# Low parts of later weights made during the feed-forwards and loaded through GpSimd's queue

## The chip, the cores and the metric

One core of one Trainium2 chip runs the kernel. Its engines work side by side, each through a queue of its own in order: TensorE (PE: matmuls; PEld is its loading of the stationary operand), VectorE (DVE), ScalarE (ACT), GpSimd (POOL) and SyncE (SP), whose queue holds nothing but DMA issues. Sixteen DMA engines move the data. The metric is the device time of one execution in microseconds (us), the median over runs.

## The reference, cut to what matters

A network of four layers over 512 tokens of width 1024, all in float32. Two layers of a first block, each with four mixers and a gated feed-forward of width 2816:

```python
for l in range(2):
    h = rms_norm(x, pre_mix_g[l]);  z = h @ w_in[l]      # z is split into 18 column groups
    o_a, o_b = hgrn2(...), gla(...)                       # chunked recurrences
    o_c, o_d = mla_attention(...), gated_delta(...)
    x = x + rms_norm(concat(o_a, o_b, o_c, o_d) @ w_out[l], post_mix_g[l])
    h = rms_norm(x, pre_ffn_g[l])
    gate = causal_dwconv(h @ ffn_w_gate[l], ffn_conv_w[l])
    x = x + rms_norm((gelu(gate) * (h @ ffn_w_up[l])) @ ffn_w_down[l], post_ffn_g[l])
```

Then a second block: layer A (differential attention, with `a_w_in`) and layer B (stick-breaking attention, with `b_w_in` and the shared `w_kv_shared`), both with a small attention to a memory. The first block's output is the second's input.

## The kernel before

Every large product is made of float32 operands that are split into a high part (rounded to the matmul's fp32r format) and a low part (what is left), and takes three matmuls, high by high, high by low and low by high (`mm3`, L817). A weight comes in **views** of 128 partitions x 1024 values (512 KB). `wload` (L799) makes one ready: SP loads the raw view into a `wr` buffer (there are two), ScalarE casts it to the high part `wh` (four buffers), and VectorE subtracts, `wl = wr - wh` (four buffers). Both the cast and the subtraction read `wr`, so the next load into that buffer waits for both. TensorE spends 24 matmuls on a view of a projection.

`layer1(l)` is a layer of the first block: norm, the projections with the mixers (GDN, HGRN, GLA, MLA) between them, the output product, then `ffn`. `ffn(l, ...)` loops over 22 column blocks f of the feed-forward: two views each (gate and up), convolution and gelu on ScalarE and VectorE, and the product with `ffn_w_down` at the end. The stages of the profile below follow this: layer 0's mixers 30 to 385 us, its feed-forward loop 385 to 604 and down product 604 to 706, layer 1's mixers 726 to 1022, its feed-forward 1072 to 1422, layer A 1440 to 1706, layer B from 1731 on.

The order of the work is not the order of the code. Every operation is recorded (`Engine`; all carry the line of its call, L328), and a planner (`Plan.simulate`) walks through them with a cost for each, and lets every engine take the ready operation that comes first in the program. The operations are then emitted in the order of their planned starts. The planner has DMAs on an engine of their own; in the emitted program a DMA stands in the queue of the engine that issues it. A load that depends on nothing can be planned far ahead if a buffer of its pool is free. The pool `p2` (128x512, ten buffers, printed as `p` or `p2`) serves the mixers and the feed-forward for temporaries. The rstd of a norm is made on GpSimd: a `TENSOR_SCALAR` and a `TENSOR_TENSOR` (a power) on `st` tiles of a few values per partition.

Of the kernel before, what the change touches and what calls it, by code (L numbers as in the profile page):

```python
# [10 lines left out]
F32 = mybir.dt.float32  # L11
F32R = mybir.dt.float32r
# [12 lines left out]
NF = DFF // 128  # L25
# [122 lines left out]
def run(gen):  # L148
    for _ in gen:
        pass  # L150
# [14 lines left out]
class Clocks:  # L165
# [4 lines left out]
    def __init__(self):  # L170
        self.T = {e: 0.0 for e in ("PE", "ACT", "DVE", "POOL", "DMA")}
        self.wrote, self.read, self.slots = {}, {}, {}
# [441 lines left out]
class Net:  # L614
    def __init__(self, ctx, tc, I, out, dbg=None, upto=None):
        self.tc, self.nc, self.I, self.out, self.dbg = tc, tc.nc, I, out, dbg
        self.upto = upto
        nc = tc.nc
        self.clk = Clocks()
        self.plan = Plan(nc)  # L620
        self.plan.skip = {a.tensor.name for a in I.values()} | {out.tensor.name}
        eng = lambda name, e: Engine(self.clk, self.plan, name, e)
        self.V, self.A, self.G = eng("DVE", nc.vector), eng("ACT", nc.scalar), eng("POOL", nc.gpsimd)
        self.PE, self.SP = eng("PE", nc.tensor), eng("DMA", nc.sync)
        self.n = 0
        pool = lambda name, bufs, **k: ctx.enter_context(tc.tile_pool(name=name, bufs=bufs, **k))
        self.pc = pool("pc", 1)
        self.bufs = {"h": 8, "p": 8, "w": 16}
        self.pools = {k: pool("p4" + k, n) for k, n in self.bufs.items()}
        self.p2_ = pool("p2", 10)  # L630
        self.pst = pool("pst", 31)
        self.pst4 = pool("pst4", 10)
        self.pwr = pool("pwr", 2)
        self.pwh = pool("pwh", 4)
        self.pwl = pool("pwl", 4)
        self.pps = {"A": pool("psA", 3, space=PSUM), "S": pool("psS", 3, space=PSUM), "D": pool("psD", 2, space=PSUM)}
        self.pdr = pool("pdr", 2, space=bass.MemoryType.DRAM)
        self.turn = 0
        self.ready_w, self.mem_kv, self.mem_hT = {}, {}, {}
        self.ahead = lambda: None  # L640

    def nm(self, s):
# [156 lines left out]
    def wload(self, view, tag=None):  # L799

        if self.wkey(view) in self.ready_w:
            return self.ready_w.pop(self.wkey(view))
        sh = list(view.shape)
        raw = self.new(self.pwr, 2, sh, F32, "wr", "wr")
        for k in range(sh[1] if len(sh) == 4 else 1):
            part = (slice(None), k) if len(sh) == 4 else slice(None)
            self.SP.dma_start(out=raw[part], in_=view[part])
        if tag:
            hi, lo = (self.p4(sh, F32R, tag) for _ in range(2))
        else:  # L810
            hi = self.new(self.pwh, 4, sh, F32R, "wh", "wh")
            lo = self.new(self.pwl, 4, sh, F32R, "wl", "wl")
        self.A.copy(hi, raw)
        self.sub(lo, raw, hi.bitcast(F32))
        return hi, lo

    def mm3(self, out, a, b, start, stop):  # L817

        self.mm(out, a[0], b[0], start, False)
        self.mm(out, a[0], b[1], False, False)  # L820
        self.mm(out, a[1], b[0], False, stop)
# [1052 lines left out]
    def ffn_views(self, l):  # L1874
        I = self.I
        return [self.cols(I[k][l], f * 128, 128) for f in range(NF) for k in ("ffn_w_gate", "ffn_w_up")]

    def ffn(self, l, h, rest, then):

        I = self.I  # L1880
        Wd = I["ffn_w_down"][l]
        views = self.ffn_views(l) + [self.out_rows(Wd, 0, 0)]
        acts = []
        first = self.fm_first(h, [self.wload(v) for v in views[:3]], rest)
        self.preload(views[3])

        def proj(i):
            if i < 3:
                return first[i]
            w = self.wload(views[i])  # L1890
            self.preload(views[i + 1])
            return self.fm(h, w)

        for f in range(NF):
            if l == 0 and f == 2:
                run(self.mem_prep(1))
            psg, psu = proj(2 * f), proj(2 * f + 1)
            c = self.p2()
            self.act(c, psg, AF.Copy, scale=self.fcols[l](f, 2))
            for j in (1, 0):  # L1900
                s = 2 - j
                self.stt(c[:, s:], psg[:, :S - s], self.fcols[l](f, j), c[:, s:], ALU.mult, ALU.add)
            self.act(c, c, AF.Gelu_apprx_tanh)
            self.mul(c, psu, c)
            a = self.p4([128, 2, S], F32R, "w" if f < 16 else "p")
            self.split(a[:, 0, :], a[:, 1, :], c)
            acts.append(a)
        gb = self.bcast_row(I["post_ffn_g"][l], D)
        self.xt = self.load_x(acts[NF - 1][:, 0, :].bitcast(F32), "w")
        return self.out_proj(Wd, lambda k, t: (acts[k][:, 0, t * 128:(t + 1) * 128], acts[k][:, 1, t * 128:(t + 1) * 128]),  # L1910
                             list(range(0, NF, 2)), lambda t, ps: self.residual_norm(t, ps, gb, "w"),
                             "SSSD", "AAAD", then, "pw")
# [636 lines left out]
```

## Time and profile before

| | |
|---|---|
| median of 3 runs (lowest, highest) | 2016.34 us (2011.52, 2017.5) |
| the profiled execution | 2016.91 us, its span 2014.8 us |
| busy share of the span | PE 97%, PEld 82%, DVE 62%, ACT 47%, POOL 13% |
| the chain that ended last | PE 84%, DVE 7%, issue 3%, POOL 2%, ACT 2%, DMA 1% |
| `DVE wl` subtractions | 296, 338.5 us in all |
| DMA traffic | 195.81 MB, 97 GB/s over the span |

The profile comes from one execution. "Busy" of an engine is the sum of its instructions' times. The chain is followed back from the last instruction, at each step to what released it; a piece of it is time that the program could not do without as it stands. "Windows" give busy times of each engine in a stretch of the span. In the names, `out<-in`, numbers of buffers are left out.

### The profile page before, as it was taken

The page shows a single profiled execution, that of the slowest core. Times are in us where ns is not written, and L with a number is a line of the kernel's source. Part 1 is how long each engine was busy: PE and PEld are TensorE (multiplying, and loading weights), DVE is VectorE, ACT ScalarE, POOL GpSimd, SP SyncE. Part 2 cuts the span into 40 slices and gives each one's busy share as a digit, 9 for nine tenths or more (in the row PEclk, how much of TensorE's full clock was granted, in tenths as well). Part 3 has the DMA queues.
Part 4 walks back from the last instruction along what each step waited for, and adds up shares of the span by engine and source line. Part 5 has one row for each costly group of instructions (what it writes and reads, how often), then busy time and mean ns, then how long its engine had stood idle before and what let it go on. Part 6 is the DMA issues. An engine that isn't in the chain of part 4 may idle for free.

```text
span 2014.8 us, 33230 instructions
## 1 busy us (share of the span) xinstructions
PE 1954.8 (97%) x13254; PEld 1660.5 (82%) x13254; DVE 1250.2 (62%) x2333; ACT 948.5 (47%) x1723; POOL 260.6 (13%) x374
## 2 busy tenths in 40 slices
PE   7999999999999999998999999999999999999999
PEld 6888777888888878886887888888899988888777
DVE  8688884544442266878745444422648886558796
ACT  6654464433331246633644333322446764457782
POOL 2201211000000021011111000000323310005141
PEclk9999999999999999998999999999999999999999
DMA  7321136333332433302253333325421213322121
GB/s 222 95 64 36 62 105 200 108 100 96 95 94 94 157 110 95 77 25 64 64 189 102 97 94 95 94 94 178 136 64 54 76 62 130 121 84 63 53 74 63
DMA packets 232457, 195.81 MB, mean 97 GB/s; under 512 B 22480, under 2 KB 201328, under 8 KB 232304
## 3 DMA queue, kind: packets, MB, share of 16 engines
q1 hardware_dynamic: 232304, 193.71, 31.1%
q8 instruction: 104, 1.70, 0.4%
q14 instruction: 49, 0.40, 0.1%
HBM read 176.37 MB, written 17.30 MB: 96 GB/s over the span
## 4 chain that ended last, share of the span: by engine, by line
PE 84%; DVE 7%; issue 3%; POOL 2%; ACT 2%; DMA 1%; SPq 0%; DVEq 0%; POOLq 0%; ACTq 0%
PE psA L328 63%; PE psS L328 13%; PE psD L328 8%; DVE p4w L328 4%; POOL st L328 2%; ACT p4w L328 1%; DVE p4p L328 1%; DVE p L328 1%; DMA wr<-in_w_in_dram 1%; DVE wl L328 0%; DVE st L328 0%; DVE p4h L328 0%; DMA p4p<-in_x_dram 0%; ACT wh L328 0%; ACT p4p L328 0%
## 5 line engine op out<-in xcount | busy, mean ns | idle before, releaser
L328 DVE TENSOR_TENSOR wl<-wr,wh 128x1024 fp32r<-128x1024 f32 (+4 forms) x296 | 338.5, 1150 | 413.1 <-ACT wh L328 408.3
L328 PE MATMUL psA<-p4h,wh 128*128 128x512 f32 (+1 forms) x1952 | 585.7, 382 | 0.2 <-ACT p4h L328 0.2
L328 ACT CAST wh<-wr 128x1024 fp32r<-128x1024 f32 (+4 forms) x296 | 290.2, 989 | 486.6 <-PE psA L328 287.7
L328 PEld LDWEIGHTS psA<-p4h,wh 128*128 128x128 f32 x1952 | 359.8, 189 | 76.1 <-issue 2.5
L328 PE MATMUL psA<-p4h,wl 128*128 128x512 f32 (+1 forms) x976 | 374.7, 384 | 0.6 <-DVE wl L328 0.6
L328 PE MATMUL psA<-wh,p4h 128*128 128x256 f32 (+1 forms) x1728 | 347.0, 292 | 0.0
L328 PEld LDWEIGHTS psA<-wh,p4h 128*128 128x128 f32 x1728 | 276.3, 190 | 5.6 <-issue 2.3
L328 PE MATMUL psA<-wl,p4h 128*128 128x256 f32 (+1 forms) x864 | 249.3, 289 | 0.0
L328 PEld LDWEIGHTS psA<-p4h,wl 128*128 128x128 f32 x976 | 184.2, 189 | 34.0 <-DVE wl L328 0.8
L328 POOL TENSOR_SCALAR st<-st 128x1 f32<-128x1 f32 (+4 forms) x114 | 37.5, 329 | 1260.9 <-ACT p4w L328 841.4
L328 PEld LDWEIGHTS psA<-wl,p4h 128*128 128x128 f32 x864 | 164.5, 190 | 1.6 <-issue 0.8
L328 PE MATMUL psA<-wh,p4w 128*128 128x512 f32 (+1 forms) x540 | 162.3, 371 | 2.4 <-DVE p4w L328 1.9
L328 ACT ACTIVATE p<-p 128x512 f32<-128x512 f32 (+2 forms) x174 | 87.2, 526 | 106.9 <-DVE p L328 105.5
L328 POOL TENSOR_TENSOR st<-st,c 128x1 f32<-128x1 f32 (+4 forms) x112 | 118.9, 1063 | 8.4
L328 ACT ACTIVATE p4w<-psA 128x256 f32<-128x256 f32 (+5 forms) x138 | 61.9, 452 | 117.3 <-PE psA L328 112.8
L328 PEld LDWEIGHTS psA<-wh,p4w 128*128 128x128 f32 x540 | 97.7, 190 | 21.2 <-DVE p4w L328 2.3
L328 PE MATMUL psA<-wl,p4w 128*128 128x512 f32 (+1 forms) x270 | 99.0, 368 | 0.0
L328 DVE TENSOR_TENSOR p<-psA,p 128x512 f32<-128x512 f32 x54 | 37.3, 691 | 98.4 <-PE psA L328 93.0
L328 PE MATMUL psS<-p4w,p4w 128*64 128x64 f32 (+9 forms) x800 | 96.3, 279 | 2.0 <-DVE p4w L328 1.8
L328 PE MATMUL psS<-wh,p4w 128*128 128x512 f32 x300 | 97.4, 395 | 0.0
L328 PE MATMUL psS<-consts,p4w 128*128 128x128 f32 (+1 forms) x448 | 68.4, 285 | 26.2 <-DVE p4w L328 17.3
L328 PEld LDWEIGHTS psS<-consts,p4w 128*128 128x128 f32 x448 | 53.3, 150 | 36.4 <-DVE p4w L328 14.9
(237 smaller groups left out, 3239.1 us busy)
## 6 DMA issues: line engine op xcount, KB each, us to landing
wr<-in_w_in_dram SPq DMA_DIRECT2D x44, 512.0 KB, 3.8
wr<-in_ffn_w_gate_dram SPq DMA_DIRECT2D x44, 512.0 KB, 3.8
wr<-in_ffn_w_up_dram SPq DMA_DIRECT2D x44, 512.0 KB, 3.8
wr<-in_ffn_w_down_dram SPq DMA_DIRECT2D x44, 512.0 KB, 3.5
wr<-in_w_out_dram SPq DMA_DIRECT2D x16, 512.0 KB, 3.9
wr<-in_a_w_in_dram SPq DMA_DIRECT2D x16, 512.0 KB, 3.8
wr<-in_b_w_in_dram SPq DMA_DIRECT2D x16, 512.0 KB, 3.9
p4w<-xd SPq DMA_DIRECT2D x12, 512.0 KB, 4.6
```

The costliest lines, as they stand in the source:

```text
L328: op.fn(*op.args, **op.kw)
```

## The change

While the feed-forward of layer l runs, a new function `low_part` makes the low parts of weights that are needed after it, and stores them in DRAM; `later(l)` lists these views: all 28 of layer 1's mixers for l = 0, and 38 of A's and B's for l = 1. Each view goes in two halves of 128x512: SP loads the raw half into a `p2` buffer, ScalarE casts it into a second, VectorE subtracts into a third, and SP stores that to the DRAM tile `lw`. `wload` of such a view later still loads the raw view and casts it on ScalarE, but the low part comes from `lw` by a DMA that is issued on GpSimd (`self.G.dma_start`) straight into `wl`, in place of VectorE's subtraction. The raw buffer then has one reader, not two. The products are the same. The counts of operations change so: `wl` subtractions from 296 to 232, 132 more subtractions and casts of half views, 132 more raw loads and 132 stores on SP, 64 loads on GpSimd (two of the views stored, both of A, are not loaded again).

```diff
--- before.py
+++ after.py
@@ -636,7 +636,7 @@
         self.pps = {"A": pool("psA", 3, space=PSUM), "S": pool("psS", 3, space=PSUM), "D": pool("psD", 2, space=PSUM)}
         self.pdr = pool("pdr", 2, space=bass.MemoryType.DRAM)
         self.turn = 0
-        self.ready_w, self.mem_kv, self.mem_hT = {}, {}, {}
+        self.ready_w, self.mem_kv, self.mem_hT, self.low = {}, {}, {}, {}
         self.ahead = lambda: None
 
     def nm(self, s):
@@ -811,8 +811,25 @@
             hi = self.new(self.pwh, 4, sh, F32R, "wh", "wh")
             lo = self.new(self.pwl, 4, sh, F32R, "wl", "wl")
         self.A.copy(hi, raw)
-        self.sub(lo, raw, hi.bitcast(F32))
+        if self.wkey(view) in self.low:
+            self.G.dma_start(out=lo, in_=self.low[self.wkey(view)])
+        else:
+            self.sub(lo, raw, hi.bitcast(F32))
         return hi, lo
+
+    def low_part(self, view):
+
+        sh = list(view.shape)
+        d = self.pdr.tile(sh, F32, tag=self.nm("lw"), name=self.nm("lw"))
+        h = sh[1] // 2
+        for j in range(2):
+            a = (slice(None), slice(j * h, j * h + h))
+            raw, hi, lo = (self.new(self.p2_, 10, [128, h] + sh[2:], dt, "p2", "p2_") for dt in (F32, F32R, F32R))
+            self.SP.dma_start(out=raw, in_=view[a])
+            self.A.copy(hi, raw)
+            self.sub(lo, raw, hi.bitcast(F32))
+            self.SP.dma_start(out=d[a], in_=lo.bitcast(F32))
+        self.low[self.wkey(view)] = d
 
     def mm3(self, out, a, b, start, stop):
 
@@ -1875,6 +1892,27 @@
         I = self.I
         return [self.cols(I[k][l], f * 128, 128) for f in range(NF) for k in ("ffn_w_gate", "ffn_w_up")]
 
+    def later(self, l):
+
+        I = self.I
+        if l == 0:
+            W = I["w_in"][1]
+            gdn, gate_d = self.gdn_items(1, W, None, None, {})
+            items = gdn + gate_d + self.hgrn_items(1, W, None, {})[0] + self.gla_items(1, W, None, {})[0] + \
+                self.mla_items(1, W, None, {}) + self.hgrn_items(1, W, None, {})[1] + self.gla_items(1, W, None, {})[1] + \
+                self.mem_items(1)
+            return [v for vs, _ in items for v in vs]
+        A, K, B = I["a_w_in_2"][0], I["w_kv_shared_2"], I["b_w_in_2"][0]
+        halves = lambda W, c: [self.cols(W, c, 256)[:, k:k + 4] for k in (0, 4)]
+        out = []
+        for g in range(1, 8):
+            out += halves(A, 1536 + g * 256)
+        for g in range(3):
+            out += halves(K, 768 + g * 256)
+        for n in range(6):
+            out += [self.cols(W, c + n * 128, 128) for W, c in ((K, 0), (B, 0), (B, 1024))]
+        return out
+
     def ffn(self, l, h, rest, then):
 
         I = self.I
@@ -1891,7 +1929,10 @@
             self.preload(views[i + 1])
             return self.fm(h, w)
 
+        todo = self.later(l)
         for f in range(NF):
+            for v in todo[f * len(todo) // NF:(f + 1) * len(todo) // NF]:
+                self.low_part(v)
             if l == 0 and f == 2:
                 run(self.mem_prep(1))
             psg, psu = proj(2 * f), proj(2 * f + 1)
```

Since the planner orders all operations anew, their places in the queues change too. First SP's queue at the start of the program. The names are tiles (`p4w`: inputs of the memory's norm, `p_945` and `st`: parameters of the second block, `wr`: raw weights) with numbers of the program's own, and `in_...` the kernel's inputs. Before:

```order
L328 DMA p4w_172<-in_mem_norm_dram 128x1024
L328 DMA p4w_176<-in_mem_dram 128x1024
L328 DMA p4w_183<-in_mem_dram 128x1024
L328 DMA p_945_1040<-in_plam_dram 128x256
L328 DMA st_1044<-in_positions_dram 128x4x1
L328 DMA wr_154<-in_wsm_dram 128x8x56
L328 DMA wr_168<-in_w_in_dram 128x8x128
L328 DMA wr_191<-in_w_in_dram 128x8x128
```

And SP's queue at the same place in the changed kernel:

```order
L328 DMA p4w_172<-in_mem_norm_dram 128x1024
L328 DMA p4w_176<-in_mem_dram 128x1024
L328 DMA p4w_183<-in_mem_dram 128x1024
L328 DMA p_715_809<-in_w_in_dram 128x4x128
L328 DMA p_718_812<-in_w_in_dram 128x4x128
L328 DMA p_725_818<-in_w_in_dram 128x4x128
L328 DMA p_728_821<-in_w_in_dram 128x4x128
L328 DMA p_739_831<-in_w_in_dram 128x4x128
L328 DMA st_1240<-in_positions_dram 128x4x1
L328 DMA wr_154<-in_wsm_dram 128x8x56
L328 DMA wr_168<-in_w_in_dram 128x8x128
```

Five raw half views for layer 1, whose casts come in layer 0's feed-forward, now stand ahead of `wsm` and of the weight `wr_168` of layer 0; the 128 KB of `plam` moved to a later place. At the end of layer 0's feed-forward five half views of `a_w_in` stand in the same way, and lie in `p2` until layer 1's feed-forward.

Second GpSimd's queue where layer 0's feed-forward ends and layer 1 begins. The `st` operations are the rstds of the two norms there for the last blocks of rows; a `TENSOR_TENSOR` makes what the `TENSOR_SCALAR` of the same chain began. Before:

```order
L328 MEMSET p4w_1333 128x1024
L328 TENSOR_SCALAR st_1179<-st_1178 128x1
L328 MEMSET p4w_1334 128x1024
L328 TENSOR_TENSOR st_1180<-st_1179,c_108 128x1
L328 TENSOR_SCALAR st_1189<-st_1188 128x1
L328 TENSOR_SCALAR st_1196<-st_1193,st_1195 128x1
L328 TENSOR_TENSOR st_1190<-st_1189,c_108 128x1
L328 TENSOR_TENSOR st_1197<-st_1196,c_108 128x1
```

GpSimd's queue at the same place in the changed kernel:

```order
L328 MEMSET p4w_1529 128x1024
L328 DMA wl_1417<-lw_808 128x1024
L328 TENSOR_SCALAR st_1375<-st_1374 128x1
L328 MEMSET p4w_1530 128x1024
L328 DMA wl_1421<-lw_817 128x1024
L328 DMA wl_1426<-lw_830 128x1024
L328 TENSOR_TENSOR st_1376<-st_1375,c_108 128x1
L328 TENSOR_SCALAR st_1385<-st_1384 128x1
L328 TENSOR_SCALAR st_1392<-st_1389,st_1391 128x1
L328 TENSOR_TENSOR st_1386<-st_1385,c_108 128x1
L328 TENSOR_TENSOR st_1393<-st_1392,c_108 128x1
```

Three loads of low parts now stand among these rstds. Each has to wait until TensorE has done with the old part in its `wl` buffer, and what stands behind it on GpSimd waits with it. At the way into A two such loads stand among the rstds, and at the way into B two ahead of one rstd and two ahead of the next.

Third GpSimd's queue at the way into B in the changed kernel, where the `st` operations are again rstds of the last blocks of rows; before, they stood one behind the other.

```order
L328 DMA wl_3423<-lw_2202 128x1024
L328 DMA wl_3426<-lw_2219 128x1024
L328 TENSOR_SCALAR st_3404<-st_3403 128x1
L328 TENSOR_TENSOR st_3405<-st_3404,c_108 128x1
L328 TENSOR_SCALAR st_3410<-st_3409 128x1
L328 TENSOR_TENSOR st_3411<-st_3410,c_108 128x1
L328 DMA wl_3456<-lw_2226 128x1024
L328 DMA wl_3459<-lw_2243 128x1024
L328 TENSOR_SCALAR st_3416<-st_3415 128x1
L328 TENSOR_TENSOR st_3417<-st_3416,c_108 128x1
```

Two rstds now stand behind two loads each. TensorE's matmuls are the same ones as before; in layer 1's mixers their order changes in many places, elsewhere hardly.

## Rows read from the trace of the kernel before

**Rows 1.** The page: busy time and share; the chain that ended last, by engine

```profile
PE 1954.8 (97%) x13254; PEld 1660.5 (82%) x13254; DVE 1250.2 (62%) x2333; ACT 948.5 (47%) x1723; POOL 260.6 (13%) x374
...
PE 84%; DVE 7%; issue 3%; POOL 2%; ACT 2%; DMA 1%; SPq 0%; DVEq 0%; POOLq 0%; ACTq 0%
```

**Rows 2.** Windows by stage: length; PE, PEld, DVE, ACT, POOL busy (count); clock; DMA share; GB/s

```profile
385.00:604.00 219.00, 219.00 (x959) 179.65 (x958) 102.11 (x119) 78.58 (x100) 0.00 (x0) 1.00 0.34 101
...
726.00:1022.00 296.00, 279.93 (x2888) 241.44 (x2887) 224.96 (x444) 151.06 (x276) 40.29 (x50) 0.95 0.26 75
...
1072.00:1318.00 246.00, 245.63 (x1140) 204.66 (x1141) 116.72 (x142) 88.99 (x118) 0.74 (x2) 0.99 0.32 97
...
1440.00:1706.00 266.00, 260.71 (x1960) 242.62 (x1959) 198.35 (x486) 155.89 (x333) 67.52 (x102) 1.00 0.27 81
...
1731.00:2005.00 274.00, 272.97 (x1558) 226.76 (x1557) 196.96 (x407) 173.84 (x357) 62.87 (x64) 1.00 0.21 66
```

**Rows 3.** The chain by line, in 726 to 1022 us, then in 1440 to 1706

```profile
by line: PE psA L328 53.6%; DVE p4w L328 14.0%; PE psS L328 10.4%; PE psD L328 8.8%; issue 2.7%; POOL st L328 2.0%; ACT p4w L328 1.6%; DVE p L328 1.3%; DMA wr<-in_w_in_dram 1.3%; DVE wl L328 1.1%; ACT wh L328 0.7%; DVE st L328 0.6%; DVE p4p
...
by line: PE psA L328 65.8%; PE psS L328 12.2%; POOL st L328 4.8%; PE psD L328 4.8%; ACT p4w L328 2.5%; issue 2.4%; DVE st L328 2.3%; POOL p4w L328 1.3%; ACT p4p L328 0.9%; DVE p4w L328 0.8%; DVE p L328 0.8%; ACT wh L328 0.7%; ACT p L328 0.5
```

**Rows 4.** Groups of the page: out<-in, form, count | busy us, mean ns | idle before

```profile
L328 DVE TENSOR_TENSOR wl<-wr,wh 128x1024 fp32r<-128x1024 f32 (+4 forms) x296 | 338.5, 1150 | 413.1 <-ACT wh L328 408.3
...
L328 ACT CAST wh<-wr 128x1024 fp32r<-128x1024 f32 (+4 forms) x296 | 290.2, 989 | 486.6 <-PE psA L328 287.7
```

**Rows 5.** The chain in order of time, 722 to 734 us: start, length, what

```profile
725.21 1.01 DVE wl L328 x4
...
726.64 3.95 DMA wr<-in_w_in_dram
...
730.61 1.04 ACT wh L328
```

**Rows 6.** The chain in layer 1's mixers, and one piece of B

```profile
841.95 5.51 PE psA L328 x24
...
910.41 0.47 DVE wl L328
...
912.65 0.60 DVE wl L328
...
1001.54 0.60 DVE wl L328
...
1849.88 1.23 DVE wl L328
```

**Rows 7.** Windows at the start, columns as in the stages

```profile
15.00:20.00 5.00, 3.84 (x18) 3.58 (x18) 3.80 (x16) 4.61 (x11) 3.99 (x5) 1.00 1.05 396
20.00:25.00 5.00, 4.99 (x41) 4.75 (x39) 4.83 (x17) 4.23 (x12) 4.67 (x6) 1.00 0.69 152
```

**Rows 8.** Waits, 1072 to 1318 us: who for whom, us in total, times, longest

```profile
ACT wh L328 <- PE psA L328: 98.3, 42, 3.8
```

**Rows 9.** The chain at the start

```profile
17.25 6.64 DMA wr<-in_w_in_dram
```

**Rows 10.** SP's queue at the start: start, length of the issue, what

```profile
15.79 0.33 SPq L328 DMA_DIRECT2D p<-in_plam_dram  x1
...
16.71 0.43 SPq L328 DMA_DIRECT2D wr<-in_wsm_dram  x1
```

**Rows 11.** GpSimd in order of time, 717 to 735 us

```profile
722.55 0.19 POOL L328 TENSOR_SCALAR st<-st 128x1 f32<-128x1 f32 x1
724.27 0.96 POOL L328 MEMSET p4w<- 128x1024 f32 x1 [1.52 <-DVE p4w L328]
...
727.14 1.86 POOL L328 TENSOR_SCALAR st<-st,st 128x1 f32<-128x1 f32 x1 [0.68 <-ACT p4w L328]
728.96 1.06 POOL L328 TENSOR_TENSOR st<-st,c 128x1 f32<-128x1 f32 x2
```

**Rows 12.** SP's queue: what it waited for, us in total, times, longest

```profile
SPq L328 <- DVE p L328: 29.8, 8, 10.9
```

## The prediction

> **What bounds the kernel now.** I read the page first, for who is busy and what the chain that ended last is made of: TensorE is busy 97% of the span and holds 84% of the chain, VectorE 7%, GpSimd 2%, transfers 1% [rows 1]. So nearly all the time is matmul time, and a change that leaves the matmuls alone can win only what TensorE does not do. Then I cut the span into its stages [rows 2]. The feed-forward loops (385 to 604 and 1072 to 1318 us) have TensorE busy to the last microsecond; VectorE is at 102.11 of 219 and 116.72 of 246 us there, the DMA engines at a third. The mixers of layer 1 (726 to 1022) are different: TensorE leaves 16.1 us of 296, and VectorE, at 224.96, is busy 76%. Layer A (1440 to 1706) leaves 5.3 us, B (1731 to 2005) 1.0. Last I read the chain inside the two stages where something is left [rows 3]: in layer 1's mixers VectorE's `p4w` (the recurrences) has 14.0%, 41 us, and `DVE wl`, the instructions that the change takes out, 1.1%, 3.3 us. In A `DVE wl` is not even in the list's head, while `POOL st`, the rstds of the norms, has 4.8%, 12.8 us. The reader is to see two sizes: 64 subtractions of some 1.2 us each are 79 us of VectorE, but of these only about 5 us stand on the chain.
>
> **The change part by part.** The sum is made against the profiled execution, 2016.91 us, which lies 0.6 us above the median of the three runs, 2016.34.
>
> *Removed: 64 subtractions* (28 in layer 1's mixers, 12 in A or kept for it, 24 in B). The group's mean is 1150 ns over all forms [rows 4]; the large form takes 1.21 to 1.23 us. On the chain they stand from 725.21 on, until at 726.64 a weight load goes out that waits for the raw buffer which they free (1.43 us) [rows 5], from 910.41 to 912.65 in three pieces (1.81 us with the middle one of 0.74), at 1001.54 (0.60), and once in B (1.23) [rows 6]. That is -5.1 us at first order. Behind it lies what other VectorE instructions gain because fewer stand ahead of them: no row prices that. Its bounds are nothing and all of TensorE's idle time of layer 1's mixers and A, 16.1 + 5.3 = 21.4 us [rows 2]. I take -3, near the lower end, because the chain puts most of those stages on TensorE itself (psA 53.6% and 65.8%) [rows 3] and the chain's VectorE part is one recurrence after the other, which wait for TensorE and not for a free VectorE.
>
> *Moved: TensorE's order in layer 1's mixers.* The matmuls are the same, their order there is planned anew. I cost it at nothing, with the same bounds as above.
>
> *Added in the feed-forwards: 132 raw loads of at most 256 KB, as many casts, subtractions and stores.* A cast or subtraction of 128x512 is half of one of 128x1024, 0.50 and 0.58 us by the means [rows 4]. For 28 views in the first loop VectorE gets 56 x 0.58 = 32 us and goes to 134 of 219; for 38 in the second 76 x 0.58 = 44, to 160 of 246. ScalarE, from 78.58 and 88.99, goes to 106 and 127. A view moves 1.05 MB (in and out): 29 MB over 219 us are 134 GB/s on top of 101, 40 MB over 246 us 162 on top of 97. The start of the kernel moves 396 [rows 7]. What hides all this is that the weights run ahead: casts of the second loop wait 98.3 us, in 42 waits, for TensorE to give buffers back [rows 8]. I take 0. If the cover went, because a queue stands still longer than three views take (24 matmuls of a view are 5.51 us [rows 6], so 16.5 us), TensorE would wait for the rest.
>
> *Added at the program's start: five raw loads of 256 KB in SP's queue, ahead of `wsm` and a first-layer weight,* where 128 KB stood. The queue is full there: 15 to 20 us runs at 396 GB/s with the DMA engines wholly busy [rows 7], and the chain goes through the weight load that is issued at 17.25 and takes 6.64 us [rows 9]. 5 x 0.262 - 0.131 = 1.18 MB at 0.396 MB/us are 3.0 us; the issues alone, four more of 0.33 to 0.43 us [rows 10], are 1.5. Bounds 0 (the later load is faster by what it no longer meets) and 3.0; I take 3.0, since the DMA engines are at work without a gap until the load lands (20 to 25: share 0.69).
>
> *Added to GpSimd: 64 DMA issues.* No row has a DMA issued there. From below: SP's issues, 0.33 to 0.43 us [rows 10]. From above: GpSimd's own slowest instruction of that neighbourhood, a 128x1 `st` of 1.86 us, where the same operation takes 0.19 when nothing disturbs it [rows 11]. I take 1.0, nearest to the `MEMSET` of 128x1024 there, 0.96 us: the work is over a tile of the same shape. What is queued behind an issue are rstds, and for them wait the norms, then the transposes, then TensorE. At the way into layer 1, three issues stand between the rstds of the last two row blocks: 3.0 us, less 1.6 us that GpSimd has in hand (it ends at 730.02, the weight's cast, which the chain takes, at 731.65) [rows 5, 11], +1.4. Into A two: 2.0, less the same slack, +0.4. Into B two and two: I count half of the four, +2.0. Inside A two pairs near the head norms, whose rstds are chain there (12.8 us), half counted: +2.0. Sum +5.8; from below 0 (0.4 an issue disappears in the slack), from above 13 issues (the nine at the three entries, the four in A) of 1.86, 24 us.
>
> *Loads in place of subtractions.* A 128x1024 part must land before its matmuls, where a 512 KB load took 3.8 us (median) and its issue waits until TensorE has left the old part in one of four buffers: 16.5 us of other views lie between, so I take 0; above, see the third rival.
>
> Sum: -5.1 - 3 + 0 + 3.0 + 5.8 = +0.7, so 2017.6 us; rounded **2018**, no change that can be told: 0.3% (6 us) is about what a measurement of this kernel can tell from no change.
>
> **The rivals.**
>
> *VectorE's relief is worth more (faster).* With 64 of 296 weight subtractions gone from stages in which VectorE is 72 to 76% busy, the recurrences come sooner, and the new order of TensorE fills what is left. For it speaks that layer 1 alone loses some 33 us of VectorE work and has 16.1 us of idle TensorE; against it that `DVE wl` is 1.1% of its chain. All 21.4 us back, less 3.0 at the start and 3.0 of GpSimd: 2016.9 - 15.4 = 2001.5 us.
>
> *GpSimd's queue becomes a link of the chain (slower).* If an issue costs what the disturbed `st` costs, 1.86 us, the 13 issues at the entries and in A put 24 us on rstds, for which everything there waits. It decides where all 13 count and one costs over 0.85 us (13 x 0.85 + 3.0 - 8.1 = 6). 2016.9 + 24 + 3.0 - 5.1 = 2039 us.
>
> *A late low part (slower).* A transfer from GpSimd's queue could make headway only while VectorE pauses. 3.8 us at a VectorE busy 76% of the time would then be 3.8/0.24 = 15.8 us. That fits into 16.5 us of other views, except where views follow each other quickly and `DVE wl` is on the chain already, at 910 to 913 and at 1001 [rows 6]: two places, each 12 us more, 2016.9 + 24 + 0.7 = 2042 us. For this speaks the row of 1.86 against 0.19 us, GpSimd held up beside a busy VectorE [rows 11]; against it that the transfer itself runs on DMA engines which have room (share 0.26) [rows 2].
> The Trainium skill says how this might be ("SBUF — State Buffer", SBUF: two separate sides): GpSimd writes the descriptors of its own transfers through a port pair that VectorE locks in some modes, so they starve beside such VectorE work. By that rule the time would be the 2042 just worked out, by the row of the transfers' room 2018; no run here shows a transfer of that queue yet.
>
> *The small buffers run short (slower).* The five early raw parts lie in five of the ten `p2` buffers until the first feed-forward takes them up, and five more through layer 1's mixers. The mixers' own temporaries then share the other five. Before, SP's queue waited for a `p` buffer's writer at most 10.9 us [rows 12]; one such wait in front of a weight gives 2016.9 + 10.9 + 0.7 = 2028.5 us.
>
> **How the numbers follow.** No change to be told 0.36, relief 0.34, GpSimd's queue 0.15, the small buffers 0.08, a late part 0.07. The first is the likeliest, hence 2018; it spills 0.02 to either side, and 0.01 of relief stays within 0.3%: faster 0.35, same 0.33, slower 0.32. Its own range is 2011 to 2025. The whole range cuts the best third of relief (0.11, below 1998) and the worst of GpSimd and late parts (0.08, above 2040): 1998 to 2040.
>
> **What would show it.** In the changed kernel: `DVE wl` x232 in place of x296, and stages 385 to 604 and 1072 to 1318 of unchanged length (the work beside them is hidden). The weight load of the start landing near 27 instead of 23.9 us. On GpSimd, what the rstds at the three entries wait, and how long an issue takes: under 0.5 us, and the slow rival is dead; near 1.9, and it is right. The mixers of layer 1, 296 us long now: below 285 the relief is real, above 300 something new waits. Wrong I would be above all if the new order there does what I cost at nothing, or if TensorE is seen waiting for `wl` from a DMA.

## The result, and the profile after

The changed kernel takes 2162.7 us (median of 4 runs, 2158.86 to 2163.58) against 2014.22 for the kernel before in the same comparison: a ratio of 1.0729, 95% interval 1.0714 to 1.0744. It is slower by 7%, far outside the predicted 1998 to 2040 us.

First the page of the changed kernel: busy shares, the chain by engine, and three groups (busy us, mean ns of one, then the engine's idle time just before them and what ended most of it).

```profile
PE 1999.6 (93%) x13254; PEld 1688.8 (78%) x13254; DVE 1270.6 (59%) x2401; ACT 1026.5 (47%) x1858; POOL 293.4 (14%) x438
...
PE 77%; DVE 9%; ACT 5%; DMA 3%; issue 3%; POOL 2%; SPq 1%; DVEq 0%; ACTq 0%; POOLq 0%
...
L328 PE MATMUL psA<-p4h,wh 128*128 128x512 f32 (+1 forms) x1952 | 615.1, 398 | 94.5 <-DVE p L328 94.5
...
L328 DVE TENSOR_TENSOR wl<-wr,wh 128x1024 fp32r<-128x1024 f32 (+4 forms) x232 | 260.6, 1132 | 348.3 <-ACT wh L328 338.6
...
L328 DVE TENSOR_TENSOR p<-p,p 128x512 fp32r<-128x512 f32 (+3 forms) x146 | 96.3, 660 | 67.0 <-DMA lw<-p 59.3
```

TensorE still has its 13254 matmuls, but is busy 1999.6 us where it was 1954.8, and its share of the chain fell from 84 to 77% [rows 1]. The subtractions of `wl` are x232, down from x296 [rows 4]: the change does what it says. New is the 94.5 us for which the matmuls `psA<-p4h,wh` waited for `DVE p`, where the same group had 0.2 us of idle time before, and the 67.0 us for which VectorE's half subtractions (`p<-p,p`) waited, mostly for the stores `lw<-p`.

Next the stages, cut at the same matmuls as before but for one start, given below (columns as in [rows 2]; the counts of PE show that each holds the same work within three matmuls).

```profile
387.00:631.00 244.00, 226.37 (x958) 183.74 (x957) 135.27 (x173) 107.33 (x151) 0.00 (x0) 0.97 0.64 193
...
756.00:1055.00 299.00, 283.08 (x2886) 243.66 (x2887) 193.23 (x412) 149.47 (x273) 51.10 (x73) 0.95 0.41 122
...
1105.00:1462.60 357.60, 278.45 (x1140) 224.90 (x1141) 160.26 (x204) 125.16 (x181) 0.74 (x2) 0.88 0.54 165
...
1584.50:1850.00 265.50, 260.73 (x1959) 242.32 (x1958) 186.03 (x473) 154.93 (x332) 71.44 (x115) 1.00 0.34 107
...
1876.00:2151.00 275.00, 273.12 (x1555) 226.80 (x1554) 171.69 (x383) 174.30 (x354) 73.26 (x84) 1.00 0.34 104
```

Held against [rows 2]: the first feed-forward loop 244.0 us for 219, the second loop 357.6 for 246, A 265.5 for 266, B 275.0 for 274. Layer 1's mixers are cut here at the first matmul behind the down product. In the kernel before none begins from 726 to 729 us, and that matmul begins at 729.00, so the row to hold against is not the 296 us of [rows 2] but this one of the trace before:

```profile
729.00:1022.00 293.00, 279.61 (x2886) 241.44 (x2887) 222.02 (x439) 150.31 (x273) 38.05 (x47) 0.95 0.26 75
```

That is 299.0 us for 293. So 25.0 + 111.6 us of loss lie in the two loops, where I had put nothing, and all the mixers together grew by some 7 us. The loops also show that a wait is paid for twice: of the 111.6 us in the second, TensorE idles 79.2 (357.6 - 278.45), and its same 1140 matmuls are busy 32.8 us longer (278.45 for 245.63), at a granted clock of 0.88 where it was 0.99, a mean between the two levels of 1.2 and 2.4 GHz.

Who TensorE waits for in the second loop, from the waits (us in total, times, longest):

```profile
PE psA L328 <- DVE p L328: 77.8, 13, 10.7
DVE p L328 <- DMA lw<-p: 45.7, 24, 4.8
```

And how such a wait comes about, from the chain in order of time (start, length, what):

```profile
1179.93 11.23 PE psA L328 x49
...
1193.40 0.69 DVE p L328
...
1194.11 4.34 DMA lw<-p
...
1198.54 0.70 DVE p L328
...
1199.27 0.70 ACT p L328
...
1199.99 0.76 DVE p L328
...
1200.78 0.76 DVE p L328
...
1201.67 13.27 PE psA L328 x47
```

TensorE stops at 1191.16 and goes on at 1201.67. In between, VectorE subtracts a low half (1193.40), SP stores it (4.34 us until it has landed), and only then does VectorE begin its next low half (1198.54), which had no buffer in `p2` until the store gave one back. Behind that instruction, in VectorE's queue and through ScalarE's copy of the gate, stand the loop's own convolution steps (`ACT p`, `DVE p` of 0.76 us), which read TensorE's psum; and there are three `psA` buffers. The store of a low part that A or B will load, at 1584 us or later, has become a link between two matmuls.

### The profile page after: what moved, and what is told of

Read it like the earlier page. It is cut to its first block, busy times and chain, and to the rows that moved or that the text cites. A ratio compares the mean times of both kernels' runs of the same rounds, so it can differ in the third digit from the quotient of the medians.

```text
span 2161.0 us, 34206 instructions
## 1 busy us (share of the span) xinstructions
PE 1999.6 (93%) x13254; PEld 1688.8 (78%) x13254; DVE 1270.6 (59%) x2401; ACT 1026.5 (47%) x1858; POOL 293.4 (14%) x438
## 4 chain that ended last, share of the span: by engine, by line
PE 77%; DVE 9%; ACT 5%; DMA 3%; issue 3%; POOL 2%; SPq 1%; DVEq 0%; ACTq 0%; POOLq 0%
PE psA L328 57%; PE psS L328 12%; PE psD L328 8%; DVE p4w L328 4%; DVE p L328 3%; POOL st L328 2%; ACT wh L328 2%; ACT p4w L328 1%; DVE wl L328 1%; ACT p L328 1%; DMA lw<-p 1%; SPq L328 1%; DVE p4p L328 1%; DVE st L328 0%; DMA dn<-p4w 0%
## 5 line engine op out<-in xcount | busy, mean ns | idle before, releaser
L328 PE MATMUL psA<-p4h,wh 128*128 128x512 f32 (+1 forms) x1952 | 615.1, 398 | 94.5 <-DVE p L328 94.5
L328 PEld LDWEIGHTS psA<-p4h,wh 128*128 128x128 f32 x1952 | 376.2, 198 | 178.8 <-issue 103.3
L328 DVE TENSOR_TENSOR wl<-wr,wh 128x1024 fp32r<-128x1024 f32 (+4 forms) x232 | 260.6, 1132 | 348.3 <-ACT wh L328 338.6
L328 PE MATMUL psA<-p4h,wl 128*128 128x512 f32 (+1 forms) x976 | 385.0, 395 | 0.2 <-DVE wl L328 0.2
L328 PEld LDWEIGHTS psA<-p4h,wl 128*128 128x128 f32 x976 | 192.4, 197 | 39.5 <-DVE wl L328 0.4
L328 DVE TENSOR_TENSOR p<-p,p 128x512 fp32r<-128x512 f32 (+3 forms) x146 | 96.3, 660 | 67.0 <-DMA lw<-p 59.3
L328 ACT CAST p<-p 128x512 fp32r<-128x512 f32 (+1 forms) x132 | 80.4, 609 | 98.8 <-DVE p L328 66.4
L328 ACT ACTIVATE p<-p 128x512 f32<-128x512 f32 (+3 forms) x174 | 87.9, 524 | 70.6 <-DVE p L328 68.5
```

The source lines that it names most:

```text
L328: op.fn(*op.args, **op.kw)
```

## The experiments

Where no number of runs is given below, a time is that of one run, and a stage's length is always that of one execution.

**Which part of the making costs?** Three theories were put against each other: too few `p2` buffers (what the chain above suggests); the added casts and subtractions themselves, in order on ScalarE and VectorE; and the added traffic. First the same work in two buffers a half in place of three:

```diff
-            raw, hi, lo = (self.new(self.p2_, 10, ... "p2", "p2_") for dt in (F32, F32R, F32R))
+            raw, hi = (self.new(self.p2_, 10, ... "p2", "p2_") for dt in (F32, F32R))
...
-            self.sub(lo, raw, hi.bitcast(F32))
-            self.SP.dma_start(out=d[a], in_=lo.bitcast(F32))
+            self.sub(raw, raw, hi.bitcast(F32))
+            self.SP.dma_start(out=d[a], in_=raw)
```

> The low part of a half view is subtracted into the raw buffer itself, so a half takes two p2 buffers and not three; transfers, casts and subtractions are the same. Theory (buffers): in the feed-forward loops VectorE stands in order before subtractions that wait for a p2 buffer, and TensorE then waits for VectorE; with two buffers a half the second loop falls from 357 us to below 300 and the whole to below 2110. Rival (work): the 76 casts and subtractions themselves put off the loop's own work; the second loop stays at 340 to 360 us. Rival (transfers): 165 GB/s in place of 97 make loads late; it stays at 340 to 360 as well.

2032.91 us, as the theory of the buffers had it. The two loops of this kernel, in windows:

```profile
391.80:610.90 219.10, 219.10 (x959) 179.79 (x958) 136.99 (x178) 109.95 (x157) 0.00 (x0) 1.00 0.70 220
1081.80:1332.10 250.30, 246.63 (x1140) 205.38 (x1140) 157.94 (x207) 123.41 (x183) 0.74 (x2) 0.99 0.72 225
```

219.1 and 250.3 us, with VectorE and ScalarE as busy as in the changed kernel (157.94 us against 160.26) and the same transfers (225 GB/s, since the loop is shorter). That rules out the work and the traffic: they are all there and cost 4 us.

Then the making without its stores:

```diff
-            self.SP.dma_start(out=d[a], in_=lo.bitcast(F32))
-        self.low[self.wkey(view)] = d
+        self.low[self.wkey(view)] = view
```

> The low parts are made, but not stored, and the later loads on GpSimd read the weight itself (the product is not the reference's). Buffers: the third buffer is free as soon as the subtraction ends, nothing waits for a store; the second loop below 290 us. Work: 340 to 360 us, as casts and subtractions are all there. Transfers: half of the added bytes are gone, about 300 us.

2045.71 us, and its loops:

```profile
391.00:610.00 219.00, 219.00 (x959) 179.65 (x958) 138.72 (x176) 108.67 (x154) 1.61 (x1) 1.00 0.54 159
1085.30:1344.90 259.60, 249.35 (x1140) 205.14 (x1140) 163.96 (x211) 127.64 (x187) 0.74 (x2) 0.99 0.55 162
```

219.0 and 259.6 us. With nothing to wait for at its end, a half gives its third buffer back at once. That is what the theory of the buffers said (below 290 us), and not the 300 us of the traffic, of which half was left.

Then the making without the loads:

```diff
-        if self.wkey(view) in self.low:
-            self.G.dma_start(out=lo, in_=self.low[self.wkey(view)])
-        else:
-            self.sub(lo, raw, hi.bitcast(F32))
+        self.sub(lo, raw, hi.bitcast(F32))
```

> The low parts are made and stored as in the change, but nothing is loaded: every weight's low part is subtracted by VectorE as before. All three theories: the loss sits in the making, so the time stays within 10 us of 2162.7, and the second loop within 15 us of 357.

2052.16 us: every theory missed here. The loops:

```profile
392.10:636.20 244.10, 227.38 (x959) 184.42 (x958) 135.29 (x173) 107.35 (x151) 0.00 (x0) 0.96 0.63 193
1101.10:1353.90 252.80, 248.56 (x1141) 206.51 (x1141) 163.19 (x211) 125.54 (x184) 0.74 (x2) 0.98 0.78 241
```

The first loses 25 us as in the changed kernel, the second only 7, although it makes the same 38 views with the same ten buffers. So the number of buffers alone does not set the loss; something about the order does. What differs can be worked out from the order of the program and the times in the trace: for each raw half the stretch from the issue of its load to the start of its cast, and so how many of the ten `p2` buffers hold, on average over a loop, a raw half that waits. In the changed kernel that is 4.6 in the first loop (25 us lost) and 7.3 in the second (112 lost); in this run 4.6 (25 lost) and 2.4 (7 lost). The planner lets the DMA queue take whatever is ready, and a raw load depends on nothing but a free buffer. So raw halves run some seven ahead, and the casts, the subtractions, the stores in flight and the loop's own temporaries share the two or three buffers that are left.

**Is it the raw halves that run ahead?** If so, ten buffers are enough once the raw halves are confined:

```diff
-        self.p2_ = pool("p2", 10)
+        self.p2_ = pool("p2", 8)
+        self.plr = pool("plr", 2)
...
+            raw = self.new(self.plr, 2, [128, h] + sh[2:], F32, "lr", "lr_")
+            hi, lo = (self.new(self.p2_, 8, ... "p2", "p2_") for _ in range(2))
```

> The raw halves get a pool of their own with two buffers, p2 keeps eight: ten in all, as in the change, and the same work. Theory (raw loads run ahead and lie in p2: a mean of 7.25 of the ten buffers hold a raw half that is not yet cast in the second loop, 4.65 in the first): confined to two, they leave p2 to the casts, subtractions and the loop's own tiles; the second loop below 260 us, the first below 225, the whole below 2045. Rival (ten buffers are too few, whoever holds them): the second loop stays above 300 us.

2043.04 us. Both loops, then A and B:

```profile
388.10:607.10 219.00, 219.00 (x958) 179.69 (x957) 126.46 (x159) 100.37 (x141) 0.00 (x0) 1.00 0.64 194
1081.00:1327.30 246.30, 245.92 (x1140) 204.97 (x1140) 156.96 (x207) 122.64 (x181) 0.74 (x2) 0.99 0.76 233
1449.30:1718.90 269.60, 260.60 (x1960) 241.90 (x1959) 186.32 (x473) 155.29 (x332) 72.50 (x115) 1.00 0.34 106
1744.80:2031.10 286.30, 278.94 (x1557) 228.84 (x1557) 174.67 (x384) 175.61 (x354) 74.61 (x84) 0.99 0.33 100
```

219.0 and 246.3 us: nothing is lost in the loops, with ten buffers, all the work and 233 GB/s. The theory holds. With eight buffers left to everything else, A is 3.6 and B 12.3 us longer than before [rows 2].

The other way round, one more buffer and nothing confined:

```diff
-        self.p2_ = pool("p2", 10)
+        self.p2_ = pool("p2", 11)
```

> The change with eleven p2 buffers and nothing else. If it is the number of buffers left beside the raw halves (about two in the second loop), a third one should take away much of the loss: second loop 270 to 310 us. If the raw loads run ahead into any buffer that there is: 330 to 357.

2136.32 us, and the loops:

```profile
386.20:605.30 219.10, 219.10 (x959) 179.76 (x958) 136.62 (x175) 107.98 (x152) 0.00 (x0) 1.00 0.71 220
1081.00:1436.80 355.80, 277.33 (x1141) 223.49 (x1141) 160.00 (x203) 124.98 (x181) 0.74 (x2) 0.88 0.54 166
```

The second loop loses as much as with ten, as said for raw loads that take any buffer there is: on average 8.2 buffers hold a waiting raw half, one more than with ten. The first loses nothing, and there the average is 2.4 (4.6 with ten buffers). Over these runs the loss follows that average where a half takes three buffers and is stored, and not the number of buffers. The average alone does not make the loss: in the run without stores it is 5.9 and 7.0 (0 and 13.6 us lost), in the one with two buffers a half 4.7 and 6.1 (0.1 and 4.3 us lost). It takes both, raw halves that fill the pool and a buffer that a store holds.

Last, the same pool for all, the same work, and only the plan held back:

```diff
             self.SP.dma_start(out=raw, in_=view[a])
+            load = self.plan.ops[-1]
+            if len(self.subs) >= 2:
+                self.plan.ops[self.subs[-2]].succs.append(load.n)
+                load.preds.append(self.subs[-2])
...
             self.sub(lo, raw, hi.bitcast(F32))
+            self.subs.append(self.plan.ops[-1].n)
```

> The change, and a raw half is planned only after the subtraction two halves before it: same work, same ten p2 buffers shared by all, only the order is another. Theory (raw halves that run ahead fill p2): both feed-forward loops back within 3 us of 219 and 246, no raw half lies through the mixers, the whole 2015 to 2026 us. Rival (three tiles a half are too many for ten buffers): second loop above 280 us.

2024.67 us (4 runs), ratio 1.0040 (1.0025 to 1.0056). The loops and layer 1's mixers between them:

```profile
384.60:603.70 219.10, 219.10 (x959) 179.83 (x958) 126.65 (x160) 99.69 (x141) 0.00 (x0) 1.00 0.64 192
728.40:1025.60 297.20, 281.25 (x2887) 242.73 (x2888) 194.54 (x413) 150.07 (x274) 50.54 (x73) 0.95 0.42 120
1076.40:1323.20 246.80, 246.42 (x1141) 205.53 (x1141) 158.16 (x208) 123.16 (x182) 0.74 (x2) 0.99 0.77 235
```

138 us come back by order alone; raw halves that wait hold 1.2 buffers on average in either loop. What is left is 9 us above the kernel before.

**What is the second half worth, the loads in place of subtractions?** With the making left out, the low parts loaded from the weights themselves:

```diff
-                self.low_part(v)
+                self.low[self.wkey(v)] = v
```

> Nothing is made in the feed-forwards; the 64 low parts come through GpSimd's queue from the weights themselves (the product is not the reference's), so this is the change's second half for nothing. My reading of the trace after (layer 1's mixers 299 us for 296, A and B the same within 1.5 us): no gain, 2010 to 2020 us. Rival (relief, masked in the change by the p2 buffers that lie held): 2005 us or less.

2018.7 us (10 runs), ratio 1.0019 (1.0009 to 1.0030): even as a gift the loads win nothing. Then neither loaded nor subtracted:

```diff
+        if self.wkey(view) in self.low and not tag:
+            hi = self.new(self.pwh, 4, sh, F32R, "wh", "wh")
+            self.A.copy(hi, raw)
+            return hi, hi
```

> Nothing is made in the feed-forwards, and the 64 low parts are neither subtracted nor loaded: the high part stands in for them (the product is not the reference's). This is the most that freeing VectorE of 64 subtractions can be worth. My reading (they are off the path): 2008 to 2016 us, at most 8 below before. Rival (relief, eaten up in the change by GpSimd's queue): 2003 or less.

2008.92 us (9 runs), ratio 0.9976 (0.9966 to 0.9986). So 79 us of VectorE work, gone for nothing, are worth 4.6 us in the order that the planner chose here (2008.92 beside 2013.56); in another order it can be more, as the last runs show. What was gained lies in layer 1's mixers, 284 us for 293 in the profiled execution:

```profile
733.20:1017.20 284.00, 275.12 (x2887) 237.71 (x2888) 193.66 (x412) 148.77 (x272) 36.76 (x48) 0.98 0.27 77
```

Each held against the kernel before of its own comparison (2018.7 beside 2015.93), the two runs lie 7 us apart: so much the loads through GpSimd take back, if the planner's two orders are worth the same, which was not shown. Is it the queue? Almost no making, and all 64 loads read one stored part of each shape, on SP:

```diff
+        if tuple(sh) in self.low:
+            self.low[self.wkey(view)] = self.low[tuple(sh)]
+            return
...
-            self.G.dma_start(out=lo, in_=self.low[self.wkey(view)])
+            self.SP.dma_start(out=lo.bitcast(F32), in_=self.low[self.wkey(view)])
```

> One low part of each shape is made in the first feed-forward and stored, and all 64 loads read that one, issued on SP and not on GpSimd (the product is not the reference's). Beside the run in which the loads come for nothing through GpSimd (2018.7 us): if GpSimd's queue costs what the ways into layer 1 and into B grew by there (3.6 and 2 us), 2010 to 2015; if the queue of the issue does not matter, 2016 to 2021.

2015.32 us (10 runs), ratio 1.0005 (0.9994 to 1.0016), beside 1.0019 (1.0009 to 1.0030) for the loads on GpSimd: the time lies between the two forecasts, and the intervals overlap. (The 3.6 us of the expectation rest on the cut at 726 us; held against the matmul at 729.00 us, the way into layer 1 is 0.7 us longer in the run with the loads as a gift.) The paced kernel settles it, since there the planner's order is the same, row by row, on every engine, and only these 64 rows move from one queue to the other (the last two lines above, in the paced kernel):

> As the paced kernel, with the 64 loads issued on SP in place of GpSimd. If GpSimd's queue is what the ways into layer 1 and B pay for: 2 to 5 us less than the paced kernel, 2012 to 2021 us. If the queue does not matter: the same within 2 us.

2015.02 us (10 runs), ratio 0.9996 (0.9984 to 1.0008), 9.65 us less than with GpSimd's queue, more than the 2 to 5 expected. Of the 6.25 us between the two profiled executions (2023.44 and 2017.19) layer 1's mixers give 5.5 (291.7 for 297.2):

```profile
728.50:1020.20 291.70, 279.23 (x2887) 241.14 (x2888) 195.25 (x413) 150.23 (x274) 37.11 (x48) 0.96 0.41 123
```

**Is there a version that beats both?** Paced, on SP, and only for layer 1:

```diff
-        todo = self.later(l)
+        todo = self.later(l) if l == 0 else []
```

> Paced, loads on SP, and only for layer 1's mixers, the one stage in which leaving the subtractions out shortened anything (12 us of 296). Candidate for a version that beats both: 2009 to 2015 us. With the loads' own cost as large as the gain: 2013 to 2018.

2009.62 us (12 runs), ratio 0.9965 (0.9953 to 0.9977): it beats both, by 0.35% and by 7%. Its mixers of layer 1:

```profile
730.40:1012.40 282.00, 272.53 (x2886) 235.21 (x2887) 193.94 (x412) 148.12 (x272) 37.18 (x48) 0.99 0.42 127
```

282.0 us for 293, at a granted clock of 0.99 for 0.95: 7.1 of the 11.0 us are the same 2886 matmuls, busy 272.53 us for 279.61, and the rest is idle time. Since each edit makes the planner choose anew, a last run took the loads away and left the subtractions in (the edit of the run without loads, on top of this kernel):

> As the kernel of run e11 (paced, layer 1's low parts only), but nothing is loaded: VectorE makes all the subtractions of layer 1's mixers as before, and the stored parts go unused. If e11's 6 us (2009.62 for 2015.57) come from the 28 subtractions that are gone: 2014 to 2019 us here, layer 1's mixers at 294 to 298 us. If they come from the new order that the planner chose: 2008 to 2012 us, the mixers at 282 to 288.

2013.4 us (12 runs), ratio 0.9995 (0.9984 to 1.0007), so its interval and that of the kernel with the loads do not meet: the 28 subtractions are worth some 4 us there by the medians (2013.4 against 2009.62, with the kernel before at 2015.5 in both comparisons), 6 by the ratios. It lies between the two forecasts. Its mixers:

```profile
728.60:1017.90 289.30, 275.82 (x2886) 238.64 (x2887) 222.06 (x439) 149.97 (x273) 38.01 (x48) 0.97 0.26 76
```

289.3 us: in these two executions 3.7 of the 11 us came with the new order and 7.3 with the subtractions. Over its runs the order alone is worth nothing that can be told.

## Why the prediction was wrong

**The step that failed** is the one on the feed-forwards: "What hides all this is that the weights run ahead [...] I take 0." I added busy times (VectorE to 160 of 246 us) and bandwidths, and both came nearly as worked out: 160.26 us in the second loop, and 225 to 235 GB/s in the runs that keep its pace, for 259. They do fit, as the runs with confined or paced raw halves show (219 and 246 us). But the cover that I named, views of weights three ahead, guards against a late weight, and no weight was late. TensorE was held by the other end, by psum that the loop's own VectorE steps had not read, and those stood in order behind a subtraction that waited for a buffer. I asked what engines and transfers have left over, and not what the ten buffers have.

**The right mechanism stood among the rivals, in the wrong place and at a wrong price.** "The small buffers run short" had the five early raw halves in mind and the mixers; I priced it at one wait of 10.9 us and gave it 0.08. The mixers lost little by them: layer 0's end came at 387.0 us for 385, and of the 6 us by which layer 1's grew the paced kernel, where two halves lie there and not five, still has 4 (297.2 us for 293). What I had seen in SP's queue at the start, five raw loads ahead of time, was the sign: the planner takes such a load whenever a buffer is free, so in the loops it does so again and again. There it met 56 and 76 halves, three buffers each.

**The other terms.** In the paced kernel, where the failed one is gone, +9.1 us was measured (2024.67 for 2015.57), and +0.7 had been forecast. *The start*: 3.0 us forecast; in the changed kernel the matmul that began at 30.0 us before begins at 31.1, so 1.1. (In the paced kernel two raw halves go ahead and not five, and nothing is lost there.) SP's queue shows the five loads of the changed kernel:

```profile
15.90 5.05 SPq L328 DMA_DIRECT2D p<-in_w_in_dram  x5
...
21.80 0.57 SPq L328 DMA_DIRECT2D wr<-in_wsm_dram  x1
22.48 6.88 SPq L328 DMA_DIRECT2D wr<-in_w_in_dram  x2
```

The load behind `wsm` goes out at 22.48 and not at 17.25 [rows 9], 5 us later, the five issues alone taking 5.05 us, but the chain does not stand before a load there any more. It goes through matmuls from 18.23 to 25.19 us, where it stood before the weight load from 17.25 to 23.89 [rows 9]:

```profile
18.23 6.96 PE psA L328 x44
```

*GpSimd*: 5.8 us forecast, 9.65 measured when the loads leave its queue. An issue takes 0.53 to 0.79 us, nearer to the lower bound than the 1.0 taken. At the way into layer 1, in the changed kernel:

```profile
750.56 0.79 POOL L328 DMA_DIRECT2D wl<-lw  x1 [1.13 <-PE psD L328]
...
752.56 0.59 POOL L328 DMA_DIRECT2D wl<-lw  x1
753.36 0.54 POOL L328 DMA_DIRECT2D wl<-lw  x1 [0.21 <-PE psD L328]
...
756.18 1.06 POOL L328 TENSOR_TENSOR st<-st,c 128x1 f32<-128x1 f32 x2
```

I had counted 1.4 us there, for rstds that come later. They hardly do: the last of them is done at 757.24 us, 24.4 us after a matmul of the down product at 732.88, and before at 730.02 [rows 11], 24.1 us after the same matmul at 705.90. What the chain takes there is a weight load, as before:

```profile
752.01 7.80 DMA wr<-in_w_in_dram
```

It goes out 1.6 us sooner after that matmul than before, since the subtractions in front of it are gone, but takes 7.80 us for 3.95 [rows 5], with the three low parts of 512 KB under way beside it. (In the run with neither loads nor subtractions, where it goes out as early, it took 4.5 us; in the paced kernel 7.6 with the low parts on GpSimd and 5.9 with them on SP.) So the first product of layer 1 begins 28.3 us after that matmul and not 26.1. That is the term *loads in place of subtractions*, which I had put at nothing: not the low part was late, but the raw weight beside it. That 2.2 us came out near the 1.4 forecast is luck.

More came inside the mixers, 5.5 us between the two paced executions, where I had counted nothing because the loads lie far ahead of their use: over the whole paced kernel GpSimd stands 228.9 us, in 42 waits, before an issue whose `wl` buffer TensorE still reads, and what is behind it on GpSimd stands as well. From the view of `wl` on GpSimd (an issue's min, median and max in ns; then its idle time before the issues, by releaser):

```profile
L328 POOL DMA_DIRECT2D wl<-lw x64: 527/540/787, 723.1 to 1898.6; - x64
...
  PE psA L328: 228.9, 42
```

That this is how the 5.5 us come about is argued from the queue; no run takes it apart, nor the 4 us by which the paced kernel on SP still lies above the run without low parts (0.5 us below the kernel before, and 4.6).

*The subtractions*: -8.1 forecast with what lies behind them; -4.6 measured when all 64 vanish for nothing. In its profiled execution A and B, with 36 of them, gave 2.1 us and lost 1.5: as the chain had shown, TensorE sets their pace.

**The rivals.** Relief (0.34) was worth 4.6 us where all 64 vanished, and nothing with 64 loads; the 6 us of the best kernel came with pacing, SP and layer 1 alone, all three at once. Its best had been worked out as 2001.5 us, and yet a third of its chance was put below 1998: no sum of the prediction reaches so far. GpSimd's queue (0.15) was priced by 1.86 us an issue on late rstds; an issue takes 0.54 (median), below the 0.85 from which this would decide, and the rstds at the first way in were 0.2 us late. A late low part (0.07) is not seen in TensorE's waits: over the whole kernel GpSimd's transfers land in 4.3 us, SP's of the same size in 4.0 (median us to landing, last column):

```profile
wl<-lw POOLq DMA_DIRECT2D x60, 512.0 KB, 4.3
wr<-in_w_in_dram SPq DMA_DIRECT2D x44, 512.0 KB, 4.0
```

By the Trainium skill ("SBUF — State Buffer", SBUF: two separate sides) they might have starved beside VectorE in some of its modes. The trace shows no starving, at 4.3 against 4.0 us, with VectorE busy two thirds of layer 1's mixers; whether such a mode was in use no view here shows. On the queue the Trainium skill says that DMAs issued on several engines run on the same sixteen DMA engines, and that issuing elsewhere saves only the issuing ("DMA: Bandwidth & Descriptors", Issuing engines are not separate DMA queues). This case's trace agrees with the first, by the 7.80 us of a weight load on SP beside three loads on GpSimd. With the second the paced pair agrees in sign; which part of its 9.65 us is the issuing, and which the waiting in front of an issue, was not measured.

## What to carry to other kernels

Work that is "hidden" needs three things in reserve: engine time, bandwidth, and buffers. Before calling it free, count how many buffers of a shared pool it holds and for how long, with the time a store takes to land, and look at what stands behind its instructions in each queue that runs in order. And where a planner hoists loads that depend on nothing, give them buffers of their own or a dependency that paces them: more buffers in the shared pool only let them run further ahead.

## What the runs showed of the hardware

TensorE's clock can stay at its lower level longer in one execution than in another, with nothing in the work to tell why. In the run with the loads as a gift, layer 0's mixers took 360.5 us in the profiled execution (355 before), though up to the end of the first feed-forward its program is the one of before, row by row on the engines that compute. From its windows:

```profile
200.00:225.00 25.00, 21.54 (x279) 16.64 (x274) 24.02 (x50) 8.91 (x15) 6.60 (x8) 0.93 0.14 44
225.00:250.00 25.00, 25.00 (x246) 20.69 (x246) 12.56 (x29) 9.10 (x21) 0.00 (x0) 0.73 0.20 64
...
230.00:240.00 10.00, 10.00 (x74) 8.84 (x75) 6.11 (x11) 3.14 (x7) 0.00 (x0) 0.57 0.49 156
```

The same stretches of the kernel before:

```profile
200.00:225.00 25.00, 21.56 (x276) 16.56 (x272) 24.01 (x49) 9.05 (x16) 6.60 (x8) 0.94 0.14 44
225.00:250.00 25.00, 25.00 (x277) 20.36 (x275) 16.77 (x44) 11.89 (x27) 3.11 (x4) 0.93 0.19 64
...
230.00:240.00 10.00, 10.00 (x114) 8.67 (x114) 8.24 (x22) 4.28 (x12) 0.00 (x0) 1.00 0.48 158
```

In both, TensorE had idled 3.4 to 3.5 of the 25 us up to 225, and in both the clock fell from 220 to 230 us (0.58 and 0.66 granted there). From 230 to 240 it was 0.57 in the one and 1.00 in the other. Over 225 to 250 that makes 0.73 in the one (between the levels of 1.2 and 2.4 GHz, so for about half of the time at the lower one) and 0.93 in the other, and 246 matmuls were done in the stretch and not 277. That is about 5 us between two executions of the same instructions, as large as the effects of the last experiments: a stage's length in one execution, like those of layer 1's mixers above, is no surer than that, and only the medians and intervals over several runs tell such effects.
